# A float32 two-layer trunk: elementwise work of GpSimd given to VectorE, a token factor moved behind a product, norm statistics asked for one slab later

## The chip, the core and the metric

The program runs on one core of a Trainium2 chip. Five engines work from queues of their own and meet at semaphores: TensorE (PE in the profile; PEld is its weight load), VectorE (DVE), ScalarE (ACT), GpSimd (POOL) and SyncE (SP), which here only issues DMAs. Each engine takes its instructions strictly in the order in which the program holds them. The metric is the device time of one execution in microseconds.

## The reference, cut to what matters

The trunk has two layers over 256 tokens of 1024 features, all in float32. In the code below the layer's parts that the change does not touch are left out.

```python
for l in range(DEPTH):
    x = x + 0.5 * swiglu(rmsnorm(x, ffn1_norm[l]), ffn1_w_gate[l], ffn1_w_up[l], ffn1_w_down[l])
    h = rmsnorm(x, mix_norm[l])
    proj = h @ w_in[l]            # attention q k v, lru x, lru gate, memory q, 3 branch gates
    ...                           # window attention, RG-LRU, memory attention
    merged = g[:, :, 0] * br_attn + g[:, :, 1] * br_lru + g[:, :, 2] * br_mem
    x = x + merged @ w_out[l]
    x = x + 0.5 * swiglu(rmsnorm(x, ffn2_norm[l]), ffn2_w_gate[l], ffn2_w_up[l], ffn2_w_down[l])
return rmsnorm(x, final_norm)

def rmsnorm(x, g):     # per token: x * (mean(x*x) + eps) ** -0.5, then times the gain
def swiglu(h, w_gate, w_up, w_down):
    return (jax.nn.silu(h @ w_gate) * (h @ w_up)) @ w_down
```

## The kernel before

Activations stay on chip with features on the 128 partitions and the 256 tokens along the free axis, so a factor that belongs to a token (the norm's R, a tile of 128 x 256 whose rows are alike; R2 is R seen twice, for a pair of feature tiles) is the same for all features and may be applied to a product's result.

All weights come as one stream of 432 slabs of eight 128 x 128 blocks (`wpack`, DMAs on SP). For each slab `prep` (L183) makes two tiles: ScalarE writes `whi`, the weights rounded to float32r (L197), and then one subtraction writes `wlo`, the rest (L199). That subtraction runs on VectorE, but on GpSimd for every fourth slab, and for two further slabs whenever `singles` has set `relief` (L193, L198). Each weight block then costs two matmuls: L223 multiplies `whi` with both halves of the activation (512 columns), L224 multiplies `wlo` with the hi half (256 columns). The sum of the two halves of the result is the product. `pair` computes two 128-feature tiles into one PSUM tile; there are three such PSUM tiles (pool `mm`).

The order of the program is made by `block` (L202) and `at` (L154). When the stream reaches the first block of a slab, `block` first writes the preparation of the slab three further on, then `tick` writes all tasks that have fallen due, then the slab's matmuls follow. `at(d, f)` puts task f d slabs later. So every engine's queue is a mixture of slab preparations and tasks in the order of emission, and an instruction that waits holds up all that stands behind it on its engine.

`join` (L261) empties a PSUM pair: ScalarE copies the lo half to SBUF at once, and one slab later VectorE adds the hi half (L266), which frees the PSUM tile. What stands behind the join depends on the stage:

- Feed-forward (`ffn`, L505): `gate` multiplies by R on VectorE (L513) and applies silu; `up` multiplies by R on GpSimd (L529; on VectorE for the last pair, L523), and two slabs later VectorE multiplies by the gate (L530). `half_step` (L555) adds half of the down product to x straight out of PSUM, two VectorE instructions for each pair (L557), right behind the product; the last pair comes as two `singles` (L551, L579).
- Mixing (`mix`, L616): `project` joins and multiplies by R, on GpSimd for the recurrent branch, its gate `yr` and the 12 gate pairs (L626), on VectorE for k, v and the queries. `conv` follows with three VectorE instructions for each feature tile (L640) and a split (L276). `lru_gates` multiplies the input gate on GpSimd (L668); `decay` clips on GpSimd (L701); `normalise` scales the softmax on GpSimd (L852); the branches' results are multiplied by their gates and added on GpSimd for the first two branches of the pairs 0 to 2 (L786, L788).
- Memory tokens are multiplied by their factor on GpSimd (L498).
- Norms (`Norm`): squares and sums of squares (`acc`, L348) follow each pair of x. `then(4, 6)` puts `rstd_a` four slabs behind the last product (PE sums `acc` over partitions, `stat`, L289, and VectorE works out the root, L293 to L303) and `rstd_b` six slabs behind it (PE spreads the factors, `rst`, L310).

Of the kernel before, what the change touches and what calls it, by code (L numbers as in the profile page):

```python
# [19 lines left out]
F32 = mybir.dt.float32  # L20
# [54 lines left out]
class Halves:  # L75
    """An operand of n tiles of features, each as its hi and its lo part, 256 tokens side by side."""
# [18 lines left out]
class Trunk:  # L95
    def __init__(self, tc, xT, memT, wpack, pk, const, outT):
        self.tc, self.nc = tc, tc.nc
        self.xT, self.memT, self.wpack, self.pkd, self.constd, self.outT = xT, memT, wpack, pk, const, outT
        self.order = []
        self.prepped = 0  # L100
        self.wtiles = {}
        self.dmaed = 0
        self.relief = 0
        self.stages = {}
        self.now = 0
        self.tasks = []
        self.uid = 0
# [46 lines left out]
    def at(self, delay, fn, *a):  # L154
        """Emit fn that many slabs of weights later."""
# [27 lines left out]
    def prep(self, n=1):  # L183
# [9 lines left out]
        relief = self.relief > 0  # L193
        self.relief -= relief
        for i in range(n):
            c = slice(i * HB * 128 // n, (i + 1) * HB * 128 // n)
            nc.scalar.activation(hi[:, c], st[:, c], AF.Copy)  # L197
            eng = nc.gpsimd if s % 4 == 3 or relief else nc.vector  # L198
            eng.tensor_tensor(lo[:, c], st[:, c], hi[:, c].bitcast(F32), op=ALU.subtract)  # L199
# [32 lines left out]
    def singles(self, nm, mk, X):  # L232
        """A pair, each product as soon as it is there, and whole."""
        self.relief = 2
# [11 lines left out]
    def two_pairs(self, nm, mk0, mk1, X, start=False):  # L246
        """Two pairs that reach for the last tiles of their operand late; at the start for each tile in turn."""
# [13 lines left out]
    def join(self, dst, ps, then=None, late=False):  # L261
        """dst = the sum of the halves; then() after it."""
# [10 lines left out]
    def split(self, src, X, k, n, delay=None):  # L273
        """src -> X's tiles k to k + n."""
# [9 lines left out]
    def rstd_a(self, parts, root=False):  # L284
        """parts[128, 256]: their sums over partitions -> (mean + eps) ** -0.5, tokens on partitions."""
# [20 lines left out]
    def rstd_b(self, r, R=None):  # L306
        """The factors by token on all partitions."""
# [8 lines left out]
    class Norm:  # L316
# [49 lines left out]
        def then(self, a, b):  # L366
            """The factors, in steps beside a product."""
# [13 lines left out]
        def when(self, f):  # L381
            """f needs R."""
# [47 lines left out]
    def lru_consts(self):  # L430
        """-8 * softplus(-lambda) and its multiples, for both layers."""
# [45 lines left out]
    def mem_norm(self):  # L477
        """The rms factors of the memory tokens, beside a product."""
# [13 lines left out]
    def mem_split(self, l):  # L492
        m = self.mem
        n = self.Norm(self, "mem_norm", l)
        for p in range(4):
            mp = m[:, 2 * p:2 * p + 2, :]
            R2 = self.Rm.unsqueeze(1).to_broadcast([128, 2, 256])
            self.at(2 * p, lambda mp=mp: self.nc.gpsimd.tensor_tensor(mp, mp, R2, op=ALU.mult))  # L498
# [5 lines left out]
    def ffn(self, l, w, norm, nxt, last=False):  # L504
# [14 lines left out]
        def up(pu, g, fp):  # L519
            u = self.s2("u")  # L520
            if fp == FT // 2 - 1:
                self.join(u, pu, late=True)
                V.tensor_tensor(u, u, norm.R2, op=ALU.mult)  # L523
# [4 lines left out]
            def rest():  # L528
                nc.gpsimd.tensor_tensor(u, u, norm.R2, op=ALU.mult)  # L529
# [15 lines left out]
        if last:  # L545
            return self.finish(n, down, h)
        for mp in range(3):
            self.half_step(self.x[:, 2 * mp:2 * mp + 2, :], self.pair("pd", down(mp), h))
            n.on_pair(self.x, mp)
        for m, ps in self.singles("pd", down(3), h):  # L550
            V.scalar_tensor_tensor(self.x[:, 6 + m, :], ps, 0.5, self.x[:, 6 + m, :], op0=ALU.mult, op1=ALU.add)  # L551
# [3 lines left out]
    def half_step(self, xp, ps):  # L555
        for i in range(2):
            self.nc.vector.scalar_tensor_tensor(xp, ps[:, :, i, :], 0.5, xp, op0=ALU.mult, op1=ALU.add)  # L557

    def finish(self, n, down, h):
        """The last product, the last norm and the result, tile after tile at the end."""  # L560
# [9 lines left out]
        for mp in range(3):  # L570
            self.half_step(x[:, 2 * mp:2 * mp + 2, :], self.pair("pd", down(mp), h))
            n.on_pair(x, mp)
            self.at(1, gain, mp)
# [462 lines left out]
```

## Time and profile before

| | |
|---|---|
| median of 3 runs | 1321.0 us (1320.8, 1321.0, 1322.96) |
| span of the profiled execution | 1322.8 us |
| PE busy | 1286.6 us, 97% |
| VectorE busy | 990.1 us, 75% |
| ScalarE busy | 751.4 us, 57% |
| GpSimd busy | 561.0 us, 42% |
| DMA moved | 232.43 MB, mean 176 GB/s |

The execution's own time is not given beside its span; the span, 1322.8 us, lies next to the slowest of the three runs, 1.8 us above the median. A matmul's end is modelled in this profile, so that a busy PE says only that a matmul was under way: what the stream of matmuls loses is read from PE's idle time and from what ended it. A busy VectorE, too, counts the time in which an instruction has begun and is held.

### The profile page before, as it was taken

Reading aid. Unit: us, or ns where it says so; the run is one execution under the profiler, and the core shown is the slowest. Engines: PE = TensorE matmul, PEld = TensorE weight load, DVE = VectorE, ACT = ScalarE, POOL = GpSimd, SP = SyncE. Lnnn points to the kernel's source line nnn. Section 1 sums busy time; section 2 is a strip of 40 time slices with the busy share of each in tenths; the row PEclk is TensorE's granted clock in tenths of the full one; section 3 lists DMA queues with packets and bytes.
Section 4 is the critical chain, followed back from the end, with each engine's and each line's share of the span. In section 5 each row is a group of like instructions: output and inputs, shape, how many; then the busy total and the mean of one; then the engine's idle time right before and its main releaser. Section 6 shows DMA issues by size and latency. Waiting matters only on the chain.

```text
span 1322.8 us, 19626 instructions
## 1 busy us (share of the span) xinstructions
PE 1286.6 (97%) x7514; PEld 1123.2 (85%) x7514; DVE 990.1 (75%) x1173; ACT 751.4 (57%) x1117; POOL 561.0 (42%) x266
## 2 busy tenths in 40 slices
PE   9999999999999989999999999999999999899997
PEld 7887798878888878888988888987888888788887
DVE  8798755898687887777568976559976888777843
ACT  6565544578578446554445655446857664555542
POOL 2453332438547524443225542334575573333321
PEclk9999999999999999999999999999999999999999
DMA  8654655555445555556556665554554554556661
GB/s 291 202 181 151 196 183 179 161 174 165 138 129 181 164 178 178 187 184 203 187 163 208 206 191 192 192 177 142 176 165 127 164 181 160 175 188 185 182 199 43
DMA packets 64750, 232.43 MB, mean 176 GB/s; under 512 B 7312, under 2 KB 7440, under 8 KB 64400
## 3 DMA queue, kind: packets, MB, share of 16 engines
q1 hardware_dynamic: 64224, 230.65, 54.6%
q8 instruction: 59, 0.97, 0.3%
q10 hardware_dynamic: 432, 0.53, 0.1%
q14 instruction: 35, 0.29, 0.1%
HBM read 230.10 MB, written 1.05 MB: 175 GB/s over the span
## 4 chain that ended last, share of the span: by engine, by line
PE 72%; DVE 16%; issue 5%; ACT 4%; POOL 2%; DMA 1%; SPq 0%; DVEq 0%; ACTq 0%; POOLq 0%
PE pd L223 9%; PE pg L223 9%; PE pu L223 9%; DVE wlo L199 6%; PE pd L224 5%; PE pg L224 5%; PE pu L224 5%; PE pgt L223 4%; PE pbr L223 3%; PE pyr L223 2%; DVE xc L640 2%; PE pgt L224 2%; ACT whi L197 2%; PE pd L243 2%; PE pd L242 2%
## 5 line engine op out<-in xcount | busy, mean ns | idle before, releaser
L199 DVE TENSOR_TENSOR wlo<-st,whi 128x1024 fp32r<-128x1024 f32 (+2 forms) x319 | 469.2, 1478 | 202.6 <-ACT whi L197 190.4
L199 POOL TENSOR_TENSOR wlo<-st,whi 128x1024 fp32r<-128x1024 f32 (+1 forms) x119 | 295.7, 2485 | 467.3 <-ACT whi L197 407.0
L197 ACT ACTIVATE whi<-st 128x1024 fp32r<-128x1024 f32 (+2 forms) x438 | 446.2, 1045 | 75.2 <-PE pd L223 51.9
L223 PE MATMUL pu<-xs,whi 128*128 128x512 f32 x640 | 228.1, 398 | 0.9 <-ACT whi L197 0.9
L223 PE MATMUL pg<-xs,whi 128*128 128x512 f32 x640 | 226.9, 397 | 0.0
L223 PE MATMUL pd<-h,whi 128*128 128x512 f32 x528 | 187.4, 399 | 2.1 <-ACT h L275 2.1
L224 PE MATMUL pu<-xs,wlo 128*128 128x256 f32 x640 | 180.5, 282 | 2.1 <-POOL wlo L199 2.0
L224 PE MATMUL pg<-xs,wlo 128*128 128x256 f32 x640 | 179.5, 280 | 0.0
L224 PE MATMUL pd<-h,wlo 128*128 128x256 f32 x528 | 148.9, 282 | 0.0
L529 POOL TENSOR_TENSOR u<-u,R 128x512 f32<-128x512 f32 x40 | 87.7, 2192 | 139.6 <-DVE u L266 105.7
L223 PEld LDWEIGHTS pu<-xs,whi 128*128 128x128 f32 x640 | 120.8, 189 | 30.0 <-ACT whi L197 1.2
L223 PEld LDWEIGHTS pg<-xs,whi 128*128 128x128 f32 x640 | 120.1, 188 | 28.5
L223 PE MATMUL pgt<-xs,whi 128*128 128x512 f32 x384 | 138.4, 403 | 0.0
L224 PEld LDWEIGHTS pu<-xs,wlo 128*128 128x128 f32 x640 | 121.6, 190 | 2.7 <-POOL wlo L199 2.7
L223 PEld LDWEIGHTS pd<-h,whi 128*128 128x128 f32 x528 | 99.8, 189 | 26.6 <-ACT h L275 2.4
L224 PEld LDWEIGHTS pg<-xs,wlo 128*128 128x128 f32 x640 | 120.9, 189 | 0.0
L224 PE MATMUL pgt<-xs,wlo 128*128 128x256 f32 x384 | 107.1, 279 | 0.0
L224 PEld LDWEIGHTS pd<-h,wlo 128*128 128x128 f32 x528 | 100.6, 190 | 0.0
L223 PEld LDWEIGHTS pgt<-xs,whi 128*128 128x128 f32 x384 | 72.1, 188 | 19.1 <-issue 2.3
L263 ACT COPY g<-pg 128x512 f32<-128x512 f32 x40 | 23.4, 585 | 96.7 <-PE pg L224 85.4
L224 PEld LDWEIGHTS pgt<-xs,wlo 128*128 128x128 f32 x384 | 72.4, 188 | 0.2
L626 POOL TENSOR_TENSOR g<-g,R 128x512 f32<-128x512 f32 x24 | 48.4, 2015 | 47.4 <-DVE g L266 47.4
(248 smaller groups left out, 2545.4 us busy)
## 6 DMA issues: line engine op xcount, KB each, us to landing
st<-wpack SPq DMA_DIRECT2D x428, 512.0 KB, 4.1
st<-wpack SPq DMA_DIRECT2D x8, 256.0 KB, 5.5
mem<-memT SPq DMA_DIRECT2D x2, 1024.0 KB, 6.0
x<-xT SPq DMA_DIRECT2D x4, 256.0 KB, 5.5
outT<-xg SPq DMA_DIRECT2D x2, 256.0 KB, 2.6
outT<-xg ACTq DMA_DIRECT2D x2, 256.0 KB, 2.8
cst<-cst SPq DMA_DIRECT2D x1, 320.0 KB, 6.4
pk<-pk SPq DMA_DIRECT2D x1, 128.0 KB, 6.0
```

The costliest lines, as they stand in the source:

```text
L197: nc.scalar.activation(hi[:, c], st[:, c], AF.Copy)
L199: eng.tensor_tensor(lo[:, c], st[:, c], hi[:, c].bitcast(F32), op=ALU.subtract)
L223: mm(both, hi, X.both(k), start=(k == 0), stop=False)
L224: mm(out[:, 0, :], lo, X.hi(k), start=False, stop=(k == n - 1))
L242: mm(out, hi, X.lo(k), start=False, stop=False)
L243: mm(out, lo, X.hi(k), start=False, stop=(k == len(blocks) - 1))
L263: self.nc.scalar.copy(dst, ps[:, :, 1, :])
L529: nc.gpsimd.tensor_tensor(u, u, norm.R2, op=ALU.mult)
L626: mult = lambda: eng.tensor_tensor(dst, dst, norm.R2, op=ALU.mult)
L640: V.scalar_tensor_tensor(xc[:, c, d:], xr[:, c, :256 - d], tap(c, 3 - d), xc[:, c, d:], op0=ALU.mult, op1=ALU.add)
```

## The change

No elementwise instruction is left on GpSimd: every slab's `wlo` is made on VectorE (`relief` is gone), and so are the products with R in `project`, the memory tokens, the input gate, the softmax scaling and the gated sums. The clip in `decay` runs on VectorE once for four feature tiles instead of once for each.

The up product is no longer multiplied by R; the factor, which is the same for all features of a token, is applied to the down product's result. `half_step` therefore joins the down product as `join` does: ScalarE copies the lo half, one slab later VectorE adds the hi half, multiplies by 0.5 and R2, and adds to x. `on_pair` (squares, splits) moves with it. For the singles there is one VectorE instruction more.

The norms' statistics are asked for with `then(5, 7)` instead of `then(4, 6)`. Comments were taken out, so line numbers shift.

```diff
@@ prep
-        relief = self.relief > 0
-        self.relief -= relief
...
-            eng = nc.gpsimd if s % 4 == 3 or relief else nc.vector
-            eng.tensor_tensor(lo[:, c], st[:, c], hi[:, c].bitcast(F32), op=ALU.subtract)
+            nc.vector.tensor_tensor(lo[:, c], st[:, c], hi[:, c].bitcast(F32), op=ALU.subtract)
@@ mem_split
-            self.at(2 * p, lambda mp=mp: self.nc.gpsimd.tensor_tensor(mp, mp, R2, op=ALU.mult))
+            self.at(2 * p, lambda mp=mp: self.nc.vector.tensor_tensor(mp, mp, R2, op=ALU.mult))
@@ ffn, up
                 self.join(u, pu, late=True)
-                V.tensor_tensor(u, u, norm.R2, op=ALU.mult)
                 V.tensor_tensor(u, u, g, op=ALU.mult)
...
             def rest():
-                nc.gpsimd.tensor_tensor(u, u, norm.R2, op=ALU.mult)
                 self.at(2, lambda: V.tensor_tensor(u, u, g, op=ALU.mult))
@@ ffn, down
-    def half_step(self, xp, ps):
-        for i in range(2):
-            self.nc.vector.scalar_tensor_tensor(xp, ps[:, :, i, :], 0.5, xp, op0=ALU.mult, op1=ALU.add)
+    def half_step(self, p, ps, norm, n, then=None):
+        V = self.nc.vector
+        xp = self.x[:, 2 * p:2 * p + 2, :]
+        d = self.s2("d")
+        self.nc.scalar.copy(d, ps[:, :, 1, :])
+
+        def add():
+            V.tensor_tensor(d, ps[:, :, 0, :], d, op=ALU.add)
+            V.scalar_tensor_tensor(d, d, 0.5, norm.R2, op0=ALU.mult, op1=ALU.mult)
+            V.tensor_tensor(xp, xp, d, op=ALU.add)
+            n.on_pair(self.x, p)
+            if then:
+                then(p)
+
+        self.at(1, add)
+
+    def half_single(self, k, ps, norm):
+        V = self.nc.vector
+        d = self.s1("d")
+        V.scalar_tensor_tensor(d, ps, 0.5, norm.R, op0=ALU.mult, op1=ALU.mult)
+        V.tensor_tensor(self.x[:, k, :], self.x[:, k, :], d, op=ALU.add)
@@ mix
-        def project(dst, ps, eng=G):
-            mult = lambda: eng.tensor_tensor(dst, dst, norm.R2, op=ALU.mult)
+        def project(dst, ps):
+            mult = lambda: V.tensor_tensor(dst, dst, norm.R2, op=ALU.mult)
...
-            G.tensor_tensor(gi[:, sl(p), :], gi[:, sl(p), :], xc[:, sl(p), :], op=ALU.mult)
+            V.tensor_tensor(gi[:, sl(p), :], gi[:, sl(p), :], xc[:, sl(p), :], op=ALU.mult)
...
-            G.tensor_scalar(ms[:, c, :], ms[:, c, :], 0.0, None, op0=ALU.max)
+            if c % 4 == 3:
+                V.tensor_scalar(ms[:, c - 3:c + 1, :], ms[:, c - 3:c + 1, :], 0.0, None, op0=ALU.max)
...
-                    eng = V if gt is gates[1] or p == 3 else G
-                    eng.tensor_tensor(t, t, gt[:, sl(p), :], op=ALU.mult)
+                    V.tensor_tensor(t, t, gt[:, sl(p), :], op=ALU.mult)
                     if acc is not None:
-                        eng.tensor_tensor(t, t, acc, op=ALU.add)
+                        V.tensor_tensor(t, t, acc, op=ALU.add)
...
-        def normalise(P, den, eng):
+        def normalise(P, den):
             V.reciprocal(den, den)
-            eng.tensor_tensor(P, P, den.unsqueeze(2).to_broadcast([128, 4, P.shape[2]]), op=ALU.mult)
+            V.tensor_tensor(P, P, den.unsqueeze(2).to_broadcast([128, 4, P.shape[2]]), op=ALU.mult)
@@ run, at all three places
-            n.then(4, 6)
+            n.then(5, 7)
```

Two places show what this does to VectorE's queue. The first is the start of the mixing stage of layer 0, from the last recurrent pair's join (`xr<-pxr`) to the join of k and v (`kv<-pkv`), behind whose PSUM tile a later product stands. Before:

```order
L266 TENSOR_TENSOR xr_2202<-pxr_2353,xr_2202 128x512
L199 TENSOR_TENSOR wlo_2447<-st_2327,whi_2446 128x1024
L640 SCALAR_TENSOR_TENSOR xc_2203<-xr_2202,pk,xc_2203 128x255
L640 SCALAR_TENSOR_TENSOR xc_2203<-xr_2202,pk,xc_2203 128x254
L640 SCALAR_TENSOR_TENSOR xc_2203<-xr_2202,pk,xc_2203 128x253
L276 TENSOR_TENSOR xcs_2204<-xc_2203,xcs_2204 128x2x256
L640 SCALAR_TENSOR_TENSOR xc_2203<-xr_2202,pk,xc_2203 128x255
L640 SCALAR_TENSOR_TENSOR xc_2203<-xr_2202,pk,xc_2203 128x254
L640 SCALAR_TENSOR_TENSOR xc_2203<-xr_2202,pk,xc_2203 128x253
L266 TENSOR_TENSOR kv_2412<-pkv_2413,kv_2412 128x512
```

The same stretch of the changed kernel, from the same join to the same join:

```order
L261 TENSOR_TENSOR xr_2204<-pxr_2355,xr_2204 128x512
L635 TENSOR_TENSOR xr_2204<-xr_2204,R_2167 128x512
L195 TENSOR_TENSOR wlo_2449<-st_2329,whi_2448 128x1024
L649 SCALAR_TENSOR_TENSOR xc_2205<-xr_2204,pk,xc_2205 128x255
L649 SCALAR_TENSOR_TENSOR xc_2205<-xr_2204,pk,xc_2205 128x254
L649 SCALAR_TENSOR_TENSOR xc_2205<-xr_2204,pk,xc_2205 128x253
L195 TENSOR_TENSOR wlo_2479<-st_2356,whi_2478 128x1024
L271 TENSOR_TENSOR xcs_2206<-xc_2205,xcs_2206 128x2x256
L649 SCALAR_TENSOR_TENSOR xc_2205<-xr_2204,pk,xc_2205 128x255
L649 SCALAR_TENSOR_TENSOR xc_2205<-xr_2204,pk,xc_2205 128x254
L649 SCALAR_TENSOR_TENSOR xc_2205<-xr_2204,pk,xc_2205 128x253
L261 TENSOR_TENSOR kv_2414<-pkv_2415,kv_2414 128x512
```

One product with R and one `wlo` have come in between. From the second recurrent pair's join on, the whole stretch before holds four `wlo`, and now six and three products with R.

The second place is behind the last product of a mixing stage, where the sums of squares (`acc`) end and VectorE takes up the statistics (`v<-stat`), which PE must have summed in between. Before:

```order
L199 TENSOR_TENSOR wlo_4579<-st_4432,whi_4578 128x1024
L348 TENSOR_TENSOR acc_4497<-acc_4497,sq_4505 128x256 x2
L199 TENSOR_TENSOR wlo_4605<-st_4462,whi_4604 128x1024
L348 TENSOR_TENSOR acc_4497<-acc_4497,sq_4584 128x256 x2
L199 TENSOR_TENSOR wlo_4651<-st_4535,whi_4650 128x1024
L293 TENSOR_SCALAR v_4658<-stat_4654 128x2
```

And now:

```order
L195 TENSOR_TENSOR wlo_4575<-st_4428,whi_4574 128x1024
L343 TENSOR_TENSOR acc_4493<-acc_4493,sq_4501 128x256 x2
L195 TENSOR_TENSOR wlo_4601<-st_4458,whi_4600 128x1024
L343 TENSOR_TENSOR acc_4493<-acc_4493,sq_4580 128x256 x2
L195 TENSOR_TENSOR wlo_4625<-st_4487,whi_4624 128x1024
L195 TENSOR_TENSOR wlo_4647<-st_4531,whi_4646 128x1024
L195 TENSOR_TENSOR wlo_4674<-st_4572,whi_4673 128x1024
L288 TENSOR_SCALAR v_4681<-stat_4677 128x2
```

Three slabs' `wlo` instead of one stand between the last sum and the statistics: one of them was on GpSimd before, one comes from the later due time.

## Rows read from the trace of the kernel before

**Rows 1.** The page's first part: busy time, share of the span, instructions of each engine.
```profile
PE 1286.6 (97%) x7514; PEld 1123.2 (85%) x7514; DVE 990.1 (75%) x1173; ACT 751.4 (57%) x1117; POOL 561.0 (42%) x266
```

**Rows 2.** PE's waits: who waited for whom, us in total, times, longest.
```profile
PE stat L289 <- DVE acc L348: 7.0, 3, 3.4
PE pq L223 <- DVE kv L266: 6.1, 2, 3.0
PE pd L223 <- ACT h L275: 2.1, 1, 2.1
PE pu L224 <- POOL wlo L199: 2.0, 1, 2.0
PE rst L310 <- DVE r L303: 2.0, 2, 1.3
PE pwo L223 <- DVE gated L266: 1.9, 2, 0.9
PE mt L917 <- POOL P L852: 1.8, 2, 0.9
```

**Rows 3.** Windows behind stalls of PE: us, busy of each engine, granted clock, DMA.
```profile
111.40:114.80 3.40, 2.99 (x10) 2.60 (x11) 3.40 (x4) 2.79 (x5) 2.58 (x2) 0.50 0.55 159
...
266.90:272.00 5.10, 5.10 (x30) 4.45 (x31) 5.03 (x8) 5.07 (x8) 0.73 (x1) 1.00 0.35 103
...
1132.10:1135.30 3.20, 3.20 (x11) 2.72 (x12) 2.42 (x13) 0.00 (x0) 0.00 (x0) 0.50 0.99 352
```

**Rows 4.** Groups by line and shape, VectorE and GpSimd: count, busy us, mean ns.
```profile
L199 DVE TENSOR_TENSOR wlo<-st,whi 128x1024 fp32r<-128x1024 f32 x311 | 465.2, 1502 | 202.6 <-ACT whi L197 190.4 <-POOL wlo L199 7.0 <-issue 4.5
L513 DVE TENSOR_TENSOR g<-g,R 128x512 f32<-128x512 f32 x44 | 65.9, 1500 | 1.5
...
L266 DVE TENSOR_TENSOR g<-pg,g 128x512 f32<-128x512 f32 x40 | 27.3, 682 | 0.9 <-ACT g L263 0.9
...
L199 POOL TENSOR_TENSOR wlo<-st,whi 128x1024 fp32r<-128x1024 f32 x117 | 292.7, 2502 | 454.8 <-ACT whi L197 407.0 <-issue 28.8 <-PE pd L243 7.6
```

**Rows 5.** VectorE in order of time, mixing stage of layer 0: start, us, what.
```profile
242.48 0.68 DVE L266 TENSOR_TENSOR xr<-pxr,xr 128x512 f32<-128x512 f32 x1
...
251.03 1.22 DVE L199 TENSOR_TENSOR wlo<-st,whi 128x1024 fp32r<-128x1024 f32 x1
252.16 2.56 DVE L640 SCALAR_TENSOR_TENSOR xc<-xr,pk,xc 128x255 f32<-128x255 f32 x3
...
264.04 0.69 DVE L276 TENSOR_TENSOR xcs<-xc,xcs 128x512 fp32r<-128x512 f32 x1
264.64 1.51 DVE L640 SCALAR_TENSOR_TENSOR xc<-xr,pk,xc 128x255 f32<-128x255 f32 x3
266.07 0.69 DVE L266 TENSOR_TENSOR kv<-pkv,kv 128x512 f32<-128x512 f32 x1
266.79 0.69 DVE L626 TENSOR_TENSOR kv<-kv,R 128x512 f32<-128x512 f32 x1
267.40 1.22 DVE L199 TENSOR_TENSOR wlo<-st,whi 128x1024 fp32r<-128x1024 f32 x1
```

**Rows 6.** VectorE in order of time behind the last norm's sums, layer 0.
```profile
480.60 2.93 DVE L348 TENSOR_TENSOR acc<-acc,sq 128x256 f32<-128x256 f32 x2
...
484.58 0.87 DVE L348 TENSOR_TENSOR acc<-acc,sq 128x256 f32<-128x256 f32 x2
```

**Rows 7.** The waits of all engines: the input gate.
```profile
POOL gi L668 <- ACT gi L667: 28.1, 6, 7.9
```

**Rows 8.** VectorE in order of time at the end of the program.
```profile
1312.61 0.42 DVE L579 SCALAR_TENSOR_TENSOR x<-pd,x 128x256 f32<-128x256 f32 x1 [6.58 <-PE pd L243]
1313.07 0.43 DVE L580 TENSOR_TENSOR sq<-x 128x256 f32<-128x256 f32 x1
```

**Rows 9.** The 512-column matmuls (L223) in two feed-forward stretches of equal length: count behind PE.
```profile
500.00:600.00 100.00, 100.00 (x285) 53.18 (x284) 1.00 0.59 187
700.00:800.00 100.00, 100.00 (x290) 53.94 (x289) 1.00 0.61 191
```

More of the change, by code (lines that the diff above doesn't have):

```diff
@@ L102, in __init__ @@
         self.dmaed = 0
-        self.relief = 0
         self.stages = {}
@@ L232, in singles @@
     def singles(self, nm, mk, X):
-        self.relief = 2
         mm = self.nc.tensor.matmul
@@ L545, in ffn, with finish @@
         if last:
-            return self.finish(n, down, h)
+            return self.finish(n, norm, down, h)
         for mp in range(3):
-            self.half_step(self.x[:, 2 * mp:2 * mp + 2, :], self.pair("pd", down(mp), h))
-            n.on_pair(self.x, mp)
+            self.half_step(mp, self.pair("pd", down(mp), h), norm, n)
         for m, ps in self.singles("pd", down(3), h):
-            V.scalar_tensor_tensor(self.x[:, 6 + m, :], ps, 0.5, self.x[:, 6 + m, :], op0=ALU.mult, op1=ALU.add)
+            self.half_single(6 + m, ps, norm)
             n.on_last(self.x, 6 + m)
         return n
-    def half_step(self, xp, ps):
-        for i in range(2):
-            self.nc.vector.scalar_tensor_tensor(xp, ps[:, :, i, :], 0.5, xp, op0=ALU.mult, op1=ALU.add)
-    def finish(self, n, down, h):
+    def half_step(self, p, ps, norm, n, then=None):
[16 more added lines that the diff above has]
+        V.tensor_tensor(self.x[:, k, :], self.x[:, k, :], d, op=ALU.add)
+    def finish(self, n, norm, down, h):
         nc, V, A, G = self.nc, self.nc.vector, self.nc.scalar, self.nc.gpsimd
@@ L570, in finish @@
         for mp in range(3):
-            self.half_step(x[:, 2 * mp:2 * mp + 2, :], self.pair("pd", down(mp), h))
-            n.on_pair(x, mp)
-            self.at(1, gain, mp)
+            self.half_step(mp, self.pair("pd", down(mp), h), norm, n, lambda p: self.at(1, gain, p))
         warm = self.sm("warm")
@@ L578, in finish @@
             xk = x[:, 6 + m, :]
-            V.scalar_tensor_tensor(xk, ps, 0.5, xk, op0=ALU.mult, op1=ALU.add)
+            self.half_single(6 + m, ps, norm)
             V.tensor_tensor(sq[:, m, :], xk, xk, op=ALU.mult)
@@ L667, in lru_gates @@
                 A.activation(gi[:, c, :], ps[:, 1, m, :], AF.Sigmoid, bias=self.vec("lru_bx", l, c))
-            G.tensor_tensor(gi[:, sl(p), :], gi[:, sl(p), :], xc[:, sl(p), :], op=ALU.mult)
+            V.tensor_tensor(gi[:, sl(p), :], gi[:, sl(p), :], xc[:, sl(p), :], op=ALU.mult)
         kv = self.ps2.tile([128, 2, 256], F32, tag="kv", name=self.name("kv"), bufs=1)
         ps = self.pair("pkv", w(C_K, 0), norm.xs)
-        project(kv, ps, V)
+        project(kv, ps)
         vt = self.ps1.tile([128, 2, 128], F32, tag="vt", name=self.name("vt"), bufs=1)
@@ L687, in mix @@
                 ps = self.pair("pcq", w(C_CQ, p - 2), norm.xs)
-            project(qcq[:, sl(p), :], ps, V)
+            project(qcq[:, sl(p), :], ps)
             lru_gates(p)
@@ L856, in win_norm @@
             V.tensor_tensor(den, den, es, op=ALU.add)
-            normalise(P[:, :, 0:128 * (qt + 1)], den, G)
+            normalise(P[:, :, 0:128 * (qt + 1)], den)
             st["w", qt, g] = P
@@ L906, in mem_norm @@
             P, den = st["m", qt]
-            normalise(P, den, G)
+            normalise(P, den)
             st["m", qt] = P
@@ L954, in run @@
             n = self.ffn(l, "ffn1", n, ("mix_norm", l))
-            n.then(4, 6)
+            n.then(5, 7)
             self.mem_kv(l)
             n = self.mix(l, n, ("ffn2_norm", l))
-            n.then(4, 6)
+            n.then(5, 7)
             last = l + 1 == DEPTH
@@ L961, in run @@
             if not last:
-                n.then(4, 6)
+                n.then(5, 7)
         assert len(self.order) == NBLK
```

## The prediction

> **What bounds the kernel now.** I read the busy shares first, then PE's waits, then the granted clock behind them, then VectorE's groups by shape, and last VectorE's queue in order of time at the places where PE waits.
>
> PE has a matmul under way for 97% of the span, VectorE is busy for 75%, GpSimd for 42% [rows 1]. So PE's stream is the bound, and only what makes that stream wait, or run slower, can be won. The list of PE's waits is short [rows 2]. The reader is to see that nearly every releaser in it is VectorE or GpSimd: the norm statistics wait 7.0 us for the sums of squares (two long waits of about 3.4 and a small one at the end), the second query product 6.1 us for the join that frees a PSUM tile (two of 3.0), and the down product, an up product, the output projection and the memory attention's transposes wait 2.1, 2.0, 1.9 and 1.8. `rst` (2.0) is waited for at the program's start and end.
>
> [...]
>
> Why are VectorE and GpSimd late? VectorE's groups tell it [rows 4]. A `wlo` takes 1502 ns in the mean, a product of g with R 1500 ns. Undisturbed, the same two shapes take 1.22 us and 0.69 us [rows 5]. The join of a PSUM half with an SBUF half, which reads one operand only from SBUF, has a mean of 682 ns, not stretched at all [rows 4]. So the instructions with two SBUF operands are held, and GpSimd works in SBUF beside them: 311 x 0.28 + 44 x 0.81 = 123 us of VectorE's busy time in these two groups alone is holding. GpSimd itself takes 2502 ns for a `wlo`, twice VectorE's undisturbed time.
>
> **The change part by part.** Prices on VectorE are from start to start, as they follow one another in its full stretch [rows 5]: a `wlo` 252.16 - 251.03 = 1.13 us, a product of 512 columns 267.40 - 266.79 = 0.61, a join with its product behind it 266.79 - 266.07 = 0.72, three convolution taps 266.07 - 264.64 = 1.43, a split 264.64 - 264.04 = 0.60.
>
> *What VectorE gets.* 117 `wlo` at 1.13 and two of half the size are 133 us. The R products (40), gated products and sums (18), memory tokens (8), input gates (8) and small softmax products (4) are 78 at 0.61, 48 us. Eight softmax products of 1024 columns cost 9 us. The down product's join has 36 instructions where there were 24, 7 us, and eight singles have one more at 0.46 (1313.07 - 1312.61 [rows 8]), 4 us. Four R products on the last up pair go, -3 us. No row shows the clip of 1024 columns on VectorE; its nearest rows are 0.69 for 512 and 1.22 for 1024 columns with two operands, so four of them cost between nothing and 5 us; I take 4, near the row of the same size. Together some 200 us. VectorE's load would then be 990 - 123 + 200 = 1067 us, 83% of 1290: it stays under PE. ScalarE gets twelve copies more and stands at 57% [rows 1]; nothing waits for them, for the down product's PSUM tile is next needed a whole product later. At nothing they are covered by ScalarE's idle time; were that gone, the weights' hi parts behind them would be late, but these are made three slabs ahead.
>
> *The k and v join.* VectorE has no idle time from 242.48 to the join at 266.07, 23.6 us [rows 5]. The changed queue has six `wlo`, six triples of taps, two splits and three joins with their products in the same stretch: 6 x 1.13 + 6 x 1.43 + 2 x 0.60 + 3 x (0.72 + 0.61) = 20.6 us. The join comes 3.0 us earlier, and the wait for it was 3.0. Both layers together: 6.1 us go. Other bound: were the `wlo` and the products to cost their stretched means, 1.50 us, the stretch would be 25.5 us and each wait 1.9 us longer.
>
> *Statistics one slab later.* A slab is eight blocks of 100 / 285 = 0.35 us [rows 9], 2.8 us. Of the 3.4 us that leaves 0.6. The same pair of sums takes 2.93 us held and 0.87 undisturbed [rows 6], another 2.1 back, and one more `wlo` stands in front of the last sum, 1.1 lost. I take the two long waits, 6.8 us, as gone; up to 1 us each may stay. What is late next is R: it arrives a slab later, and g waits for it in SBUF. PE is not behind it, since `join` has already freed the PSUM tile.
>
> *The other waits.* The up product's late `wlo` was GpSimd's (2.50 against 1.22 us); so was the softmax product before the memory transposes. The down product waited for h, whose chain loses one product with R, 0.72 us, and its holding. The output projection waited for a gated join that stood behind held instructions. I take 2.1 + 2.0 + 1.9 + 1.8 = 7.8 us as gone, and between 0 and 4 us of it may stay.
>
> *New waits.* The input gate's product waited on GpSimd 28.1 us for ScalarE, up to 7.9 at once [rows 7]. On VectorE it holds up the next `wlo` and joins. The end nearest to the rows: VectorE comes there out of a full stretch, late itself, and the slabs up to three ahead stand in front of it in its queue. It may cost 0 to 28 us; I take 1 for all new waits.
>
> *The end.* One instruction more stands between the last product and the last statistics, 0.46 us on the path [rows 8].
>
> *The clock.* If the stalls of 2 us and more go, the five falls go: 8.5 us. The trace is not strict on it: behind the wait of 3.0 us for the k and v join in layer 0 the clock stayed at 1.00 [rows 3]. [...] Were the falls not tied to the gaps, the sum would be 8.5 us higher.
>
> *The sum.* 1322.8 - 6.1 - 6.8 - 7.8 - 8.5 + 0.5 + 1 = 1295.1 us of span. The span lies 1.8 us above the median of the runs, so against 1321.0 I forecast 1293 us.
>
> One thing beside it moves the time and is not in the change. The same pair of matmuls runs at two paces: 285 blocks in 100 us in one feed-forward, 290 in another, at the full clock [rows 9], 1.7%, about 3 us over the 180 us of a feed-forward. I cannot tell which pace the new program takes where; I allow 5 us to either side.
>
> **Rivals.**
>
> *The falls of the clock stay* though the stalls go. For it: a gap without a fall. Against it: all five falls stand behind gaps. 1293 + 8.5 = 1301 us.
>
> *Stalls for stalls.* VectorE gets the mixing stage's work and was already full there for 24 us on end [rows 5], so that joins and `wlo` are late at other places. Half of the 20.7 us of waits comes back, and with it half of the falls: 1293 + 10 + 4 = 1307 us.
>
> *The input gate.* All 28.1 us of its waiting fall on PE, as VectorE holds the joins back: 1293 + 28 = 1321, no change. Against it: the lead of three slabs.
>
> *VectorE becomes the bound.* This is the slower side. If the stretching is not GpSimd's doing but VectorE's own (a late semaphore, say), it does not end with GpSimd's work. Then `wlo` and products cost 1.50 us also on VectorE: 990 + 119 x 1.50 + 78 x 1.50 + 20 = 1305 us, and it has no weights to prepare at the start and the end, some 30 us: 1335 us. It decides as soon as the mean `wlo` stays above about 1.4 us. For it: only that no row shows GpSimd wholly absent. Against it: the unstretched join, whose one SBUF operand sets it apart [rows 4].
>
> **How the numbers follow.** Forecast 0.70, falls stay 0.09, stalls for stalls 0.10, input gate 0.04, VectorE the bound 0.07. The likeliest case alone reaches from 1286 (all small waits go, the faster pace more often) to 1301. Up to 1309 the second and third case come in; what lies above or below, about 0.17, is left out: 1284 to 1309. About 0.2% (2.6 us) is what a measurement of this kernel can tell from no change. Faster by more: the first three cases, 0.89. Within it: most of the input gate's, 0.04. Slower: 0.07.
>
> **What the changed profile would show.** Right: the mean `wlo` on VectorE near 1.22 us and g with R near 0.69; VectorE near 1050 us busy; no `stat` or `pq` row above 1 us among PE's waits; no window at 0.50 between start and end. Wrong: a mean `wlo` above 1.4; a join of a branch pair or of a query as a new releaser of PE; VectorE waiting for the input gate with PE waiting behind it; falls of the clock without a stall.

## The result, and the profile after

The changed kernel takes 1286.3 us in the median of four runs (1285.73 to 1286.35), beside 1321.98 us for the kernel before (1320.8 to 1326.26): a ratio of 0.972, 95% interval 0.970 to 0.974. Timed again in another comparison it took 1286.18 us (0.9724, 0.9708 to 0.974). The profiled execution spans 1284.3 us, 38.5 us less than the one before; the medians lie 35.7 us apart. Of all executions reported here one, of the run with the late statistics, took 4450.18 us; it is left out of that run's time below.

The first part of the page of the changed kernel: busy time, share of the span, instructions.

```profile
PE 1269.7 (99%) x7514; PEld 1116.4 (87%) x7514; DVE 980.7 (76%) x1398; ACT 758.8 (59%) x1129; POOL 0.3 (0%) x5
```

Against [rows 1], PE is busy for 99% of a shorter span. VectorE has 225 instructions more and is busy for 9 us less.

All waits of PE in the changed kernel: who waited for whom, us in total, times, longest.

```profile
PE rst L305 <- DVE r L298: 1.8, 2, 1.3
PE pq L219 <- ACT xcs L270: 1.5, 2, 0.8
PE stat L284 <- DVE sq L589: 1.3, 1, 1.3
PE warm L393 <- DVE zero L390: 1.2, 1, 1.2
PE pgu L219 <- ACT whi L194: 1.1, 1, 1.1
PE stat L284 <- DVE acc L343: 0.5, 1, 0.5
PE wt L877 <- ACT P L910: 0.4, 2, 0.2
PE pgu L220 <- DVE wlo L195: 0.2, 1, 0.2
```

They add up to 8.0 us. The rows of [rows 2] are 22.9 us, and before there were nine more, 6.9 us, of which these five are no longer listed (PE's waits, kernel before):

```profile
PE pgu L223 <- DVE xs L329: 1.0, 1, 1.0
PE pu L223 <- ACT whi L197: 0.9, 1, 0.9
PE pbr L223 <- DVE g L266: 0.9, 2, 0.4
PE pcq L223 <- DVE qcq L266: 0.8, 2, 0.5
PE pgu L223 <- DVE x L800: 0.6, 2, 0.3
```

The first of them has not gone: the first product of the program now waits at the same place for `whi`, 1.1 us. So the waits went from 29.8 to 8.0 us, 21.8 less. The groups by line and shape on VectorE, changed kernel (count, busy us, mean ns, then idle time in front):

```profile
L195 DVE TENSOR_TENSOR wlo<-st,whi 128x1024 fp32r<-128x1024 f32 x428 | 519.4, 1221 | 252.9 <-ACT whi L194 252.8
L508 DVE TENSOR_TENSOR g<-g,R 128x512 f32<-128x512 f32 x44 | 30.4, 692 | 1.5
...
L261 DVE TENSOR_TENSOR g<-pg,g 128x512 f32<-128x512 f32 x40 | 27.3, 683 | 0.0
...
L343 DVE TENSOR_TENSOR acc<-acc,sq 128x256 f32<-128x256 f32 x46 | 19.4, 422 | 1.1
```

A `wlo` takes 1221 ns instead of 1502 and a product with R 692 instead of 1500; the join, with one operand in PSUM, is what it was, 683 ns against 682 [rows 4].

The 512-column matmuls (L219) in three stretches of 100 us of the feed-forwards, changed kernel (us, busy and count of PE and of the weight load, granted clock, DMA share, GB/s):

```profile
500.00:600.00 100.00, 100.00 (x290) 53.97 (x289) 1.00 0.60 193
700.00:800.00 100.00, 100.00 (x289) 53.89 (x289) 1.00 0.60 190
1150.00:1250.00 100.00, 100.00 (x290) 53.92 (x289) 1.00 0.60 190
```

Before, the first of these three had 285, the second 290 [rows 9], and the third (the same view, kernel before):

```profile
1150.00:1250.00 100.00, 100.00 (x284) 53.18 (x284) 1.00 0.60 185
```

Two of the three long feed-forwards behind the first changed to the faster pace. Start to start, a pair of matmuls takes 346.7 ns at that pace and 353.3 ns at the other; over the 434 pairs that follow the norm's factors in a feed-forward this is 2.9 us, 5.7 for two.

The span and the mean granted clock, kernel before and, in the next fence, the changed kernel:

```profile
core 0: 1322.8 us, clock 0.991
```

```profile
core 0: 1284.3 us, clock 0.997
```

From 6.0 us to 1275.7 us, where the tail begins, no stretch at 0.50 is left: the five of which [rows 3] shows two, each 3.4 us long, are gone, by my estimate 5 x 1.7 = 8.5 us.

### The profile page after: what moved, and what is told of

Read it like the earlier page. It is cut to its first block, busy times and chain, and to the rows that moved or that the text cites. A ratio compares the mean times of both kernels' runs of the same rounds, so it can differ in the third digit from the quotient of the medians.

```text
span 1284.3 us, 19477 instructions
## 1 busy us (share of the span) xinstructions
PE 1269.7 (99%) x7514; PEld 1116.4 (87%) x7514; DVE 980.7 (76%) x1398; ACT 758.8 (59%) x1129; POOL 0.3 (0%) x5
## 4 chain that ended last, share of the span: by engine, by line
PE 90%; DVE 5%; ACT 2%; issue 1%; DMA 1%; SPq 0%; DVEq 0%; ACTq 0%
PE pg L219 11%; PE pu L219 11%; PE pd L219 9%; PE pgt L219 6%; PE pu L220 6%; PE pg L220 6%; PE pd L220 5%; PE pbr L219 4%; PE pgt L220 3%; DVE wlo L195 2%; PE pyr L219 2%; PE pbr L220 2%; PE pxr L219 2%; PE pwo L219 2%; PE pgu L219 2%; PE pd L238 2%
## 5 line engine op out<-in xcount | busy, mean ns | idle before, releaser
L195 DVE TENSOR_TENSOR wlo<-st,whi 128x1024 fp32r<-128x1024 f32 (+2 forms) x438 | 524.6, 1206 | 252.9 <-ACT whi L194 252.8
L219 PE MATMUL pg<-xs,whi 128*128 128x512 f32 x640 | 225.4, 394 | 0.0
L219 PE MATMUL pu<-xs,whi 128*128 128x512 f32 x640 | 225.2, 394 | 0.0
L219 PE MATMUL pd<-h,whi 128*128 128x512 f32 x528 | 184.1, 393 | 0.0
L220 PE MATMUL pd<-h,wlo 128*128 128x256 f32 x528 | 148.0, 280 | 0.0
L219 PEld LDWEIGHTS pg<-xs,whi 128*128 128x128 f32 x640 | 119.9, 187 | 27.2
L219 PEld LDWEIGHTS pu<-xs,whi 128*128 128x128 f32 x640 | 119.8, 187 | 27.0
L219 PE MATMUL pgt<-xs,whi 128*128 128x512 f32 x384 | 139.1, 405 | 0.0
L219 PEld LDWEIGHTS pd<-h,whi 128*128 128x128 f32 x528 | 98.9, 187 | 22.5
L219 PEld LDWEIGHTS pgt<-xs,whi 128*128 128x128 f32 x384 | 72.1, 188 | 19.5 <-issue 3.0
L270 ACT ACTIVATE h<-u 128x512 fp32r<-128x512 f32 x44 | 27.8, 632 | 46.0 <-DVE u L523 43.8
L320 ACT ACTIVATE xs<-x,pk 128x256 fp32r<-128x256 f32 x40 | 18.7, 504 | 60.8 <-DVE x L557 21.6
L238 PE MATMUL pd<-h,wlo 128*128 128x256 f32 x176 | 49.8, 283 | 0.0
```

What stands on the lines that cost most here:

```text
L195: nc.vector.tensor_tensor(lo[:, c], st[:, c], hi[:, c].bitcast(F32), op=ALU.subtract)
L219: mm(both, hi, X.both(k), start=(k == 0), stop=False)
L220: mm(out[:, 0, :], lo, X.hi(k), start=False, stop=(k == n - 1))
L238: mm(out, lo, X.hi(k), start=False, stop=(k == len(blocks) - 1))
L270: hi = lambda: self.nc.scalar.activation(X.hi(k, n), src, AF.Copy)
L320: self.t.nc.scalar.activation(self.xs.hi(k), x[:, k, :], AF.Copy, scale=self.t.vec(self.v, self.l, k))
```

## The experiments

**One half of the move at a time.** First, every `wlo` on VectorE and all else as before:

```diff
-            eng = nc.gpsimd if s % 4 == 3 or relief else nc.vector
+            eng = nc.vector
```

> The kernel before with one edit: every slab's wlo on VectorE, the rest of GpSimd's work left where it was (about 260 us of it). Theory (holding: VectorE's instructions with two SBUF operands stand still while GpSimd reads SBUF): GpSimd's 117 wlo of 2.5 us are the larger half of the holding, so the mean wlo on VectorE falls from 1.50 to about 1.30 us, the late wlo of the up product (2.0 us) and the fall of the clock behind it go, the waits for the k and v join shrink from 3.0 to under 1.5, and the time is 1298 to 1312 us. Rival (VectorE's lateness is its own): the mean wlo stays at 1.50, VectorE gets 117 x 1.5 = 175 us more and PE waits more: 1325 to 1340 us.

Measured: 1310.66 us, 0.9885 (0.9858 to 0.9913), within the theory's range, with a mean `wlo` of 1290 ns on VectorE. Second, the rest of GpSimd's elementwise work on VectorE, but one `wlo` in four still on GpSimd:

```diff
-                nc.gpsimd.tensor_tensor(u, u, norm.R2, op=ALU.mult)
+                V.tensor_tensor(u, u, norm.R2, op=ALU.mult)
...
-        def project(dst, ps, eng=G):
+        def project(dst, ps, eng=V):
```

> The kernel before with all elementwise work of GpSimd but the wlo moved to VectorE; each fourth wlo stays on GpSimd, the factor stays on the up product, the statistics stay at then(4, 6). Theory (holding): GpSimd still reads SBUF for 300 us, so wlo on VectorE keeps a mean of about 1.40 us, while VectorE has some 70 us more to do; the two long waits for the statistics stay near 3 us, the one for the softmax product goes: 1312 to 1326 us, hardly a change. Rival (what made PE wait was GpSimd as a slow producer, not the holding): the waits for GpSimd's products go with them and the time falls to 1300 to 1308 us.

Measured: 1307.1 us, 0.987 (0.9852 to 0.9889), with a mean `wlo` of 1444 ns. The theory's range was missed and the rival's met, although the holding of the `wlo` stayed. PE's longest waits in the run with every `wlo` on VectorE:

```profile
PE stat L289 <- DVE acc L348: 3.6, 3, 1.5
PE pq L223 <- ACT xcs L275: 2.8, 2, 1.4
PE pd L223 <- DVE h L276: 2.6, 1, 2.6
PE pbr L223 <- DVE g L266: 2.5, 2, 1.3
```

and the longest in the run with the rest on VectorE:

```profile
PE stat L289 <- DVE acc L348: 6.8, 2, 3.4
```

In the first of them the sums of squares are no longer held (423 ns in the mean, before 602), but GpSimd's products still stand in the chains to h and to the branches; one of u with R takes it 2078 ns there, where VectorE takes 692 for one of g in the changed kernel. In the second the chains to the branches are free (no `pwo`, `mt`, `pbr` or `pu` row is left) and the wait for h is down to 1.1 us, while the statistics wait for their sums as long as before. So there were two ways in which GpSimd cost time, and I had weighed mainly the holding: it was also a slow link in chains on which PE waits. The second run does not separate the two fully, since it also takes GpSimd's busy time from 561.0 to 310.0 us, and with it some of the holding. The two halves won 12.6 and 16.2 us.

**The two other parts alone, on the kernel before.** The token factor behind the down product:

```diff
-                nc.gpsimd.tensor_tensor(u, u, norm.R2, op=ALU.mult)
...
+            V.scalar_tensor_tensor(d, d, 0.5, norm.R2, op0=ALU.mult, op1=ALU.mult)
+            V.tensor_tensor(xp, xp, d, op=ALU.add)
```

> The kernel before with only the token factor of the up product moved behind the down product (no R product on u; the down product joined by ScalarE and three VectorE instructions, one slab later). It takes 88 us of reading off GpSimd and adds 8 us to VectorE. Theory: the wait of the down product for h in layer 0 (2.1 us) and the fall of the clock behind it (1.7 us) go, the end gets 0.5 us longer, the long waits for the statistics and for the k and v join stay at 3 us and more: 1315 to 1322 us. If the factor is the main part of the gain, the time is below 1305 us.

Measured: 1316.24 us, 0.994 (0.9925 to 0.9956), within the theory's range; no `pd` row is left among PE's waits. The late statistics:

```diff
-            n.then(4, 6)
+            n.then(5, 7)
```

> The kernel before with only then(5, 7) in place of then(4, 6). A slab is 2.8 us, so of the two waits of 3.4 us for the sums of squares 0.6 each stays, and the two falls of the clock behind them go: 1322.8 - 5.6 - 3.4 = 1314 us of span, 1311 to 1315 us in time. All other waits stay. Rival (PE only waits later, at rst or at the next join): 1318 us or more, with a new row of PE waiting behind the norm.

Measured: 1315.71 us, 0.9948 (0.9929 to 0.9968), 0.7 us above the theory's range. The waits at the statistics fell from 7.0 to 1.4 us as they should; part was given back, since `rst` waited longer (PE's waits of that run):

```profile
PE rst L310 <- DVE r L303: 3.9, 3, 1.3
...
PE stat L289 <- DVE acc L348: 1.4, 3, 0.6
```

The four parts alone won 12.6 + 16.2 + 7.0 + 7.6 = 43.4 us, more than all together: they take away some of the same waits, and two of them take the same 40 products with R off GpSimd.

**The middle part left out of the change.** Nothing on GpSimd and late statistics, but R stays on the up product, on VectorE, and the down product goes straight into x as before. The line by which its up product differs from the changed kernel's:

```diff
             def rest():
+                V.tensor_tensor(u, u, norm.R2, op=ALU.mult)
                 self.at(2, lambda: V.tensor_tensor(u, u, g, op=ALU.mult))
```

> The change without its middle part: nothing on GpSimd and the statistics one slab later, but the up product is multiplied by R on VectorE (some 40 products of 512 columns more, about 24 us of VectorE's time) and the down product goes straight into x. Theory (that part is worth what h's shorter chain and the earlier freeing of the PSUM tiles spare, one wait of about 2 us, since VectorE is far from full): 1286 to 1291 us. Rival (the parts depend on each other, and VectorE cannot take the products with R beside all else): 1295 to 1306 us.

Measured: 1287.52 us, 0.9736 (0.9721 to 0.9751), beside 1286.18 us for the changed kernel in the same comparison. Once GpSimd is out of the chain, the moved factor is worth 1.3 us by the medians, which the overlapping intervals cannot tell from nothing, and not the 7.0 it won alone.

**Does GpSimd hold VectorE?** The changed kernel, and on every odd slab GpSimd does work that nobody waits for: once with two SBUF operands, once (the control) nearly without reading.

```diff
+            if n == 1 and s % 2 == 1:
+                h = hi.bitcast(F32)
+                nc.gpsimd.tensor_tensor(self.junk, h, h, op=ALU.subtract)
```

> The changed kernel, and on every odd slab GpSimd subtracts the slab's hi part from itself into a spare tile of 1024 columns; nobody waits for that tile, but GpSimd is busy again for some 216 x 2.5 = 540 us, as it was before (561). One staging buffer is given up to make room. Theory (GpSimd's reading of SBUF holds VectorE's two-operand instructions): the mean wlo on VectorE rises from 1.22 to 1.4 us or more, VectorE's busy time from 981 to above 1130 us, waits of PE for VectorE's sums, joins or wlo come back, and the time is 1295 to 1325 us. Rival (before was slow because GpSimd delivered late what others waited for; holding is a side matter): no one waits for GpSimd here, so within 4 us of the changed kernel, 1283 to 1290.

```diff
+            if n == 1 and s % 2 == 1:
+                h = hi[:, 0:4].bitcast(F32)
+                nc.gpsimd.tensor_tensor(self.junk[:, 0:4], h, h, op=ALU.subtract)
+                for _ in range(2):
+                    nc.gpsimd.memset(self.junk, 0.0)
```

> Control for the run with the added subtraction: the same staging buffers, the same waits of GpSimd for the slab's hi part, but it reads only 4 columns of it and then writes the spare tile twice with a memset of 1024 columns. Theory (it is GpSimd's reads with two SBUF operands that hold VectorE): mean wlo stays near 1.22 us and the time within 4 us of the changed kernel, 1283 to 1290. Rival (any work of GpSimd in SBUF, or the lost staging buffer, does it): mean wlo above 1.3 us, and a time nearer to that of the other run than to the changed kernel's.

Measured: 1457.81 us with the reads, 1.1018 (1.1001 to 1.1034), far above the range, and 1300.36 us with the writes, 0.9829 (0.9813 to 0.9845). The groups of the run with the reads:

```profile
L195 DVE TENSOR_TENSOR wlo<-st,whi 128x1024 fp32r<-128x1024 f32 x428 | 624.7, 1474 | 132.5 <-ACT whi L194 132.5
L198 POOL TENSOR_TENSOR junk<-whi 128x1024 f32<-128x1024 f32 x214 | 525.7, 2457 | 908.9 <-ACT whi L194 906.3
...
L346 DVE TENSOR_TENSOR acc<-acc,sq 128x256 f32<-128x256 f32 x46 | 47.8, 1038 | 1.1
...
L264 DVE TENSOR_TENSOR g<-pg,g 128x512 f32<-128x512 f32 x40 | 27.2, 680 | 0.0
```

and two places of its order in time, VectorE:

```profile
469.36 4.05 DVE L195 TENSOR_TENSOR wlo<-st,whi 128x1024 fp32r<-128x1024 f32 x2
...
477.92 2.92 DVE L195 TENSOR_TENSOR wlo<-st,whi 128x1024 fp32r<-128x1024 f32 x1
```

beside GpSimd's, the same run:

```profile
469.85 2.48 POOL L198 TENSOR_TENSOR junk<-whi 128x1024 f32<-128x1024 f32 x1 [4.15 <-ACT whi L194]
477.78 1.97 POOL L198 TENSOR_TENSOR junk<-whi 128x1024 f32<-128x1024 f32 x1 [5.45 <-ACT whi L194]
```

The `wlo` that runs into GpSimd's subtraction is held: two take 4.05 us where two in a row take 2.35 undisturbed, one takes 2.92 instead of 1.22, both 1.7 us more, beside subtractions of 2.48 and 1.97 us. The join is untouched, 680 ns in the mean against 683. One wait for GpSimd is on record here, 0.6 us of ScalarE, and yet VectorE is busy for 1285.0 us instead of 980.7 and PE waits at almost every stage. The chain that ended last lies on VectorE for 50% of the span and on PE for 27%, where it was 5% and 90% in the changed kernel. The holding is shown, and with it that VectorE, given all the work, became the bound in this run, in which GpSimd goes on reading: the slower rival, with its condition met (mean `wlo` 1474 ns) and at a higher price than I gave it.

The control was 14 us slower than the changed kernel and missed its range, but not by what the rival said: the mean `wlo` is 1221 ns. The integer shift in the statistics' root, two columns wide, on VectorE, with GpSimd's memsets (groups):

```profile
L200 POOL MEMSET junk<- 128x1024 f32 x428 | 409.6, 957 | 25.0
...
L298 DVE TENSOR_SCALAR t<-v 128x2 int32<-128x2 int32 x7 | 6.1, 873 | 0.2
```

In the changed kernel it takes 0.17 us; VectorE there, in order of time:

```profile
472.10 0.17 DVE L293 TENSOR_SCALAR t<-v 128x2 int32<-128x2 int32 x1
```

The factors come later for it; PE's row of the control:

```profile
PE rst L310 <- DVE r L303: 5.0, 6, 1.3
```
Six of the control's seven shifts take 986 to 995 ns, each with a memset beside it; the seventh, with none, takes 169. So a memset on GpSimd (0.96 us in the mean) leaves the `wlo`, the products with R and the sums, which have two SBUF operands, as they are in the changed kernel (1221, 692 and 423 ns, there 1221, 692 and 422) and holds this shift, which has one. GpSimd's subtraction held the `wlo`, 1474 ns in the mean; why the memsets hold the shift, 873 ns in the mean against 170, and not the `wlo`, no run shows. The control's `rst` waited in front of each of the three long feed-forwards, and all three ran at the slower pace; the first:

```profile
500.00:600.00 100.00, 100.00 (x284) 53.17 (x283) 1.00 0.61 194
```

That is 3 x 2.9 = 8.7 us of its 14; its `rst` and `stat` waits are 3.6 us more than the changed kernel's.

**What sets the pace?** The changed kernel with the due times of the norms altered:

```diff
-            n.then(5, 7)
+            n.then(4, 6)
```

> The changed kernel with both due times of the norms back at (4, 6). In its trace the last sum of squares ends at 466.6 us and the statistics start at 469.0; a slab (2.8 us) earlier PE would wait about 0.5 us at two places, some 1 us in all, not 3.4 each as before. Theory A (the later due time is worth little once VectorE is not held, and the place of the spread of the factors, rst, has no part in the matmuls' pace): 1286 to 1290 us, feed-forwards still at 347 ns a pair. Theory B (the place of rst sets the pace of the product behind it): two or three of the three long feed-forwards fall back to 353 ns a pair, 2.9 us each, so 1290 to 1297 us with no wait above 1 us at the statistics.

and with `n.then(4, 7)`:

> The changed kernel with the statistics asked for at the old place and the factors spread (rst) at the new one, due times (4, 7). Together with the run at (4, 6) it separates the two places. Theory A (the place of rst has no part in the pace): the same time as the run at (4, 6), within 1.5 us. Theory B (it does): the feed-forwards keep 347 ns a pair, and the time is 1286 to 1289 us, 3 to 9 us below the run at (4, 6).

Measured: 1289.97 us (1284.98 to 1293.73; 0.9742, 0.9717 to 0.9767) and 1293.44 us (1290.81 to 1294.1; 0.9771, 0.9755 to 0.9787). At (4, 6) the statistics wait little, as expected; PE's row of the place in layer 0:

```profile
467.85 0.60 PE L284 MATMUL stat<-cst,acc 128*128 128x1 f32 x4 [0.34 <-DVE acc L343]
```

Neither theory holds as I stated it. At (4, 6) one of the three long feed-forwards is slow, against theory A (the two others have 290):

```profile
1150.00:1250.00 100.00, 100.00 (x284) 53.18 (x283) 1.00 0.60 188
```

With `rst` at its new place, (4, 7), two of the three are slow, against theory B:

```profile
500.00:600.00 100.00, 100.00 (x284) 53.18 (x283) 1.00 0.60 190
700.00:800.00 100.00, 100.00 (x290) 54.02 (x289) 1.00 0.62 194
1150.00:1250.00 100.00, 100.00 (x284) 53.18 (x283) 1.00 0.59 188
```

The fast one is the one in front of which PE waits for nothing. The two medians lie 3.5 us apart, but the executions overlap and the two profiled spans, 1288.9 and 1288.8 us, do not differ, so that the times alone do not decide between the two due times. Then the changed kernel unaltered, and with added interruptions in the stream:

```diff
+                self.t.at(1, self.again)
...
+                self.t.nc.tensor.matmul(ps[:, 128 * t:128 * t + 128], self.t.ones, self.t.ident, start=True, stop=True)
```

> The changed kernel, unaltered, timed again beside the next three. In its trace the three long feed-forwards behind the first all ran at 346.7 ns a pair of matmuls; with the statistics' due times altered, five executions of one program lay between 1285 and 1294 us, which looks as if the pace were drawn anew in each execution. If the pace is fixed by the program: 1286 us in all executions, within 1 us, as before. If it is drawn: executions between 1283 and 1297 us, in steps of about 3 us (2.9 us is one feed-forward at the other pace).

> The changed kernel, and in every feed-forward, one slab behind the spread of the norm's factors, two more small matmuls of constants (128 x 128 columns each, some 0.45 us as rst takes) into a spare PSUM tile that nobody reads. PE waits for nothing there. Theory A (a short interruption by other matmuls, even without a wait, is where the pace changes): behind it the feed-forwards run at the other pace, the three fast ones at 353 ns a pair, so 1290 to 1298 us. Theory B (the pace changes only where something is waited for, or where the place in the program sets it): 1286 + 4 x 0.45 = 1287 to 1289 us and no change of pace at the added matmuls.

Measured: 1286.18 us, with executions at 1284.3, 1284.5, 1286.2, 1286.5 and 1286.8; and 1287.99 us (0.9736, 0.972 to 0.9752) with the added matmuls, which is theory B: no feed-forward changed its pace at them; the three long ones have 290, 290 and 289 pairs in the same 100 us. The unaltered kernel lies between my two expectations, at two times 2 us apart. In its profile here, a span of 1282.4 us, the first feed-forward runs faster than in the other profile:

```profile
80.00:180.00 100.00, 99.15 (x287) 53.33 (x286) 1.00 0.61 195
```

Beside it the first profile of the same program:

```profile
80.00:180.00 100.00, 100.00 (x284) 53.18 (x284) 1.00 0.61 191
```

That feed-forward has short waits in it in both; the three others run at the fast pace in both, 289 or 290 pairs in 100 us.

**A better version?** Two small edits aimed at that first feed-forward:

```diff
-        self.at(11, n.a)
+        self.at(12, n.a)
...
+            if self.v == "ffn1_norm" and self.l == 0:
+                self.t.at(2, self.again)
```

> The changed kernel with two small edits that its trace points to: the memory norm's statistics one slab later (PE waited 0.8 us there), and two small matmuls of constants in the first feed-forward alone, two slabs behind the spread of its factors, as that feed-forward runs at 353 ns a pair from 22 to 181 us. If the interruption turns the pace there: up to 3 us less, 1282 to 1285 us. If not: 1285 to 1287 us, as the changed kernel.

Measured: 1286.5 us, 0.9729 (0.9713 to 0.9745): no change. The wait for the memory norm's sums went, and its `rst`, due as before, waited in its place (PE's waits of that run):

```profile
PE rst L305 <- DVE r L298: 3.1, 2, 1.8
```

Behind it, from 80 to 180 us, the feed-forward ran at the slow pace, 284. At the added matmuls, 34 us into the program, the stream ran at 346.7 ns a pair already, so that this run does not show whether they can turn the slow pace. None of these runs beats the changed kernel.

## Why the prediction was right, and where not

The forecast was 1293 us, the likeliest case from 1286 to 1301 and the whole range from 1284 to 1309; the time is 1286.3. The mechanism is the one that I called likeliest: the waits and the falls of the clock behind them went. But the time lies at the fast end, and what carried it there was above all the pace, for which I had an allowance and no forecast; that it fell to the fast side was luck. The sum for the span, 1295.1, was 10.8 us above the 1284.3 measured. The items below compare the two profiled executions. The spans of these are 38.5 us apart, the medians 35.7: in every later run the time lies 1.7 to 2.2 us above the span of the same execution, so that the profiled execution of the kernel before took some 1324.7 us by my estimate, and was one of the slower ones.

- *The waits.* Forecast: 6.1 + 6.8 + 7.8 gone, 1.5 added, 19.2 net. Measured: 21.8. The k and v join gave 1.5 us less than forecast. More than that came from the other side: four of the five small rows above, 3.2 us, which I left uncounted, and the 1 us set aside for new waits, for no new wait of PE came but 0.5 us at the end.
- *The k and v join.* The stretch from the second recurrent pair's join to this one was put at 20.6 us. VectorE in order of time, changed kernel:

```profile
234.26 0.68 DVE L261 TENSOR_TENSOR xr<-pxr,xr 128x512 f32<-128x512 f32 x1
...
255.48 0.68 DVE L261 TENSOR_TENSOR kv<-pkv,kv 128x512 f32<-128x512 f32 x1
```

  It is 21.2 us, with 0.5 us idle in it. So the wait shrank by 2.3 us and not 3.0, and 0.75 us stayed at each of the two places; the profile names ScalarE's `xcs` as what ended it, 0.13 us behind the end of the join. Of 6.1 us, 4.6 went.
- *The statistics.* The last sums take 0.88 us for a pair, none held, and end 2.4 us before PE asks:

```profile
465.73 0.88 DVE L343 TENSOR_TENSOR acc<-acc,sq 128x256 f32<-128x256 f32 x2
```

  The 6.8 us went as forecast. But I gave most of it to the later due time, and it was not needed for that: at (4, 6) with all of GpSimd's work gone the wait is only 0.34 us at each place. Either part alone does most of it, since on the kernel before the later due time left 1.4 us of 7.0.
- *The clock.* All five falls went, as in the sum; the rival in which they stay falls. The 8.5 us of the sum are an estimate from the trace of the kernel before: five stretches of 3.4 us at a granted clock of 0.50, of which I count half as lost. Its trace has six waits of PE of 2.0 us or more: a fall lies at five of them (2.0, 2.1, 3.0, 3.4 and 3.4 us), none at the sixth, of 3.0 us. In the changed kernel the longest wait is 1.3 us, and no fall lies inside the stream. What makes the clock fall is not shown by this: that the falls would go with the waits was my estimate.
- *The pace.* I set no value on it and allowed 5 us to either side. It gave 5.7 us, the largest part of the surplus. Waits (21.8), falls (8.5) and pace (5.7) make 36.0 of the 38.5 us; the other 2.5 us I cannot assign to a cause; by the times at which the statistics start they lie in the two mixing stages.
- *VectorE's load.* Forecast 1067 us, measured 980.7. The work added was some 200 us, so 990 + 200 - 981 = 209 us of holding went by this estimate, not the 123 of the two groups that I had counted: the sums (602 ns in the mean, now 422), the splits (of `xcs` 1238, now 684) and the other products (of u with the gate 769, now 684) were held too. Shape by shape, the instructions of the kernel before took 215 us longer than the same ones at the changed kernel's medians. This is the term that was most mis-sized, and it changed nothing, as VectorE was not the bound.
- *The input gate.* VectorE waits for it 5.3 us, 2.6 at once, and no row of PE has it behind it: its cost is hidden. VectorE's waits:

```profile
DVE gi L677 <- ACT gi L676: 5.3, 2, 2.6
```

- *The end.* One instruction more, forecast at 0.46 us: from 1273.14 to 1273.60.

```profile
1273.14 0.42 DVE L567 SCALAR_TENSOR_TENSOR d<-pd,R 128x256 f32<-128x256 f32 x1 [5.13 <-PE pd L238]
1273.60 0.42 DVE L568 TENSOR_TENSOR x<-x,d 128x256 f32<-128x256 f32 x1
```

- *The signs.* The mean `wlo` (1221 ns), g with R (692 ns) and the clock came as I had said for a right forecast. Two signs did not: the `pq` row still has 1.5 us in total, and VectorE is 981 us busy and not near 1050. A `stat` row of 1.3 us is left as well, at the end of the program, where it was 0.9.

## What to carry to other kernels

When a group of equal instructions has a mean well above its shortest member (here a `wlo`, 1502 ns against 1.22 us), look at what the neighbour engine does in that time, and sum the excess over all groups, not the two largest. Work taken off such a neighbour may cost its new engine less than nothing: here 200 us more of work left VectorE 9 us less busy. A part that wins 7 us alone may win next to nothing beside the others, so parts are priced with the others in place.

## What the hardware showed that I had not expected

- Behind the norm's factors the stream of matmuls kept one of two paces here, 346.7 or 353.3 ns a pair at the full clock, to the end of the feed-forward, and which one went mostly with whether PE had to wait in front. I took the mean time of a pair in the three long feed-forwards of 13 profiles (all but that with the added reads, which waits everywhere). In 22 of the 39, PE waited neither for the statistics nor for the factors in front; all 22 ran at 346.7 ns. In the other 17 it waited there 0.3 us or more; 14 ran at 353.3 ns and 3 at 346.7. A wait of 0.34 us can thus go with a loss of 2.9 us behind it. That the executions of one program lie up to 8.75 us apart at (4, 6), where two of the three feed-forwards have such a wait, fits; the pace of an execution without a profile cannot be read.
- The wait itself is not needed for a turn, though: the pace turns at `rst` also where PE waits for nothing. In the changed kernel the stream runs at 353.3 ns a pair in front of this `rst`, and at 346.7 behind it:

```profile
475.09 0.60 PE L305 MATMUL rst<-cst,r 128*128 128x128 f32 x4
```

  In 36 of the 39 `rst` itself did not wait. Its first matmul started 350 to 352 ns behind the start of the last 512-column matmul in all 25 of them that then ran fast, and 344 to 347 or 361 ns behind it in all 11 that ran slow; in the three others (the control's) it waited 0.67 us, and they ran slow. At the slow pace three pairs in a row take 350, 361 and 349 ns, so that a wait in front, or another number of pairs, changes where in this rhythm `rst` falls. Why that should decide is open: no run moved `rst` alone by single pairs, so that this is a match in the traces and not a tested cause. It does not hold for any interruption: the added matmuls, which started 347 or 348 ns behind the last 512-column one in feed-forwards that ran fast, turned none.
- A memset on GpSimd, which reads nothing, held a two-column shift on VectorE from 0.17 to 0.87 us in the mean of seven.
